# Making the low part of the MLP's downward weights with an accumulating DMA instead of VectorE

## The chip, the cores and the metric

One core of one Trainium2 chip runs the whole program. The metric is the time of one execution in microseconds, as the device measures it; several runs are made and the median is given. A profile of one further execution shows what each engine did and when.

## The reference

One inference step of a decoder trunk with two layers, for a prompt of 512 tokens and 8 samples of 4 new tokens each (544 token columns in all), model width 1024. Layer 0 mixes tokens by sparse attention, layer 1 by retention, and each layer ends in an MLP:

```python
def sqrelu_mlp(h, w1, w2):
    return jnp.square(jax.nn.relu(h @ w1)) @ w2
...
        yp = yp + sqrelu_mlp(rms_norm(yp, ln_mlp[i]), mlp_w_in[i], mlp_w_out[i])
        ys = ys + sqrelu_mlp(rms_norm(ys, ln_mlp[i]), mlp_w_in[i], mlp_w_out[i])
```

`mlp_w_in` is 1024 x 4096 and `mlp_w_out` is 4096 x 1024 for each layer, all in float32.

## The kernel before

All values are float32, while the matmuls read a rounded format, `fp32r`. To keep precision each operand is split in two: a high part, the value rounded to `fp32r`, and a low part, the value minus its high part. A product is then three matmuls: high by high, high by low, low by high. For weights these parts are called `wh` and `wl` (for the upward weights of the later chunks `sh` and `sl`), for activations `hs` or `xs`.

**The MLP.** The hidden width of 4096 is cut into 8 chunks of 512. For each chunk the upward product makes 512 hidden rows, which are squared, split and kept in `H[c]`; the downward product takes them back to 1024 rows and adds those to the residual `x` (L640). The upward product of chunk 0 uses plain blocks, that of the other chunks uses `fast_block`, which needs fewer products (its matmuls are at L554). The downward product of a chunk is `dense4`: two calls of `block`, 512 columns each, and each gives two units of 256 columns. So a chunk has four downward units, called here its **first to fourth quarter**. One quarter is 48 matmuls at L490: two tiles of 128 columns, for each four steps along the hidden rows, and in each step four matmuls on `wh` and then two on `wl`. The units of a chunk stand in this order: first half of the next chunk's upward product, quarters one and two, second half of the upward product, quarters three and four. After the last chunk's upward product only quarters are left.

**A quarter's weights.** One load of 1 MB (`raw`, L462, issued by SP) brings the weights of two quarters. `split_w` then takes a quarter's view of `raw`: ACT copies it into `wh` (L449), and VectorE subtracts `wh` from it into `wl` (L450). `wh` and `wl` have two buffers each (`bufs=2`). So the split of a quarter can start only when TensorE has finished the quarter two before it. `raw` has four buffers; one is free for the next load when the split of its second view is through.

**Who sets the order.** `run` hands out the split of a unit ahead of its matmuls, by a lead of about 9 us of estimated TensorE time, and a scheduler then puts each engine's instructions in one fixed order. Each engine runs its list in that order and waits on semaphores. TensorE too waits in order: where a `wl` is late, everything behind that matmul is late.

POOL has little to do in the MLP: at the end of a layer it adds up squares for the next norm (L396, L398).

Of the kernel before, what the change touches and what calls it, by code (L numbers as in the profile page):

```python
# [26 lines left out]
FT = mybir.dt.float32  # L27
# [3 lines left out]
AF = mybir.ActivationFunctionType  # L31
OP = mybir.AluOpType
# [111 lines left out]
def decoder_step(ctx, tc, x_prompt, x_sample, cache_k, cache_v, cache_kidx, state_ret, page_table,  # L144
# [5 lines left out]
    V, A, G, PE, SY = nc.vector, nc.scalar, nc.gpsimd, nc.tensor, nc.sync  # L150
# [9 lines left out]
    def ps_mm():  # L160
        return psum.tile([128, 2, 512], FT, name="mm", tag="mm")
# [7 lines left out]
    def raw_tile():  # L169
        return wp.tile([128, 2048], FT, name="raw", tag="raw", bufs=4)  # L170

    def open_main(st, name, early, hs=None):
        pool = st.enter_context(tc.tile_pool(name=name, bufs=1))
        PS.update(main=pool, early=early, hs=hs or (pool, "hs", 16))
        return pool
# [5 lines left out]
    def hs_tile(dt=FR):  # L181
        return row_tile("hs", dt)
# [14 lines left out]
    def halves(ps, rows=slice(0, 128)):  # L197
        return ps[rows, :, :HALF] if len(ps.shape) == 3 else two(ps[rows])

    def two(ap):  # L200
        return ap.rearrange("p (c n) -> p c n", c=2)
# [45 lines left out]
    def settle():  # L247
        while follow or held:
            release()
            more()  # L250
# [129 lines left out]
    def start_norm(columns=False, then=None):  # L380
        norm["pending"] = True
        follow.append(finish_norm(columns, then))
# [40 lines left out]
    def combine(i, gi):  # L423

        lo, hi = slice(0, HALF), slice(HALF, T)
        x0, x1 = hs_tile(FT), hs_tile(FT)
        for k, x in ((2 * i, x0), (2 * i + 1, x1)):
            A.activation(x, xT[k], AF.Identity, scale=gains[:, gi * 8 + k:gi * 8 + k + 1])
        n, t = hs_tile(FT), hs_tile(FT)
        V.tensor_tensor(t[:, lo], x1[:, hi], x0[:, hi], op=OP.subtract)  # L430
        V.tensor_tensor(n[:, lo], x0[:, lo], x0[:, hi], op=OP.subtract)
        yield 0.9
        V.scalar_tensor_tensor(n[:, hi], n[:, lo], -1.0, x1[:, hi], op0=OP.mult, op1=OP.subtract)
        V.scalar_tensor_tensor(t[:, hi], n[:, hi], -1.0, x1[:, lo], op0=OP.mult, op1=OP.subtract)
        yield 0.9
        for src, names in ((t, ("t3", "t4")), (n, ("n1", "n2"))):
            h, l = xs_tile(), xs_tile()
            split_into(h, l, src)
            XC[i].update({names[0]: (h[:, lo], l[:, lo]), names[1]: (h[:, hi], l[:, hi])})
            yield 0.8  # L440


    def split_w(view, eng):
        nk, cols = view.shape[1], view.shape[2]
        wh = wp.tile([128, 1024], FR, name="wh", tag="wh", bufs=2)
        wl = wp.tile([128, 1024], FR, name="wl", tag="wl", bufs=2)
        h = wh[:, :nk * cols].rearrange("p (k c) -> p k c", k=nk)
        l = wl[:, :nk * cols].rearrange("p (k c) -> p k c", k=nk)
        A.activation(h, view, AF.Copy)  # L449
        eng.tensor_tensor(l, view, h.bitcast(FT), op=OP.subtract)  # L450
        return h, l

    def block(src, k0, nk, c0, cols, xs, evac, m=128, eng=None):


        raw = {}

        def view():
            if "v" not in raw:
                t = raw_tile()  # L460
                raw["v"] = t[:, :nk * cols].rearrange("p (k c) -> p k c", k=nk)
                SY.dma_start(raw["v"], src[128 * k0:128 * (k0 + nk), c0:c0 + cols]  # L462
                             .rearrange("(k p) c -> p k c", p=128))
            return raw["v"]
        per = max(1, min(cols // m, 8 // nk))

        def unit(u):
            got = {}

            def split():  # L470
                got["w"] = split_w(view()[:, :, m * per * u:m * per * (u + 1)], eng or V)
                yield nk * per * m / 128 * 0.75

            def parts():
                xx = xs() if callable(xs) else xs
                for t in range(per):
                    yield from tile_of(got["w"], xx, t, m, evac, per * u + t)
            return dict(load=view, split=split, parts=parts, rest=lambda: [])
        return [unit(u) for u in range(cols // (m * per))]

    def tile_of(hl, xs, t, m, evac, i):

        ps = ps_mm()
        n = len(xs)
        for k in range(n):
            xh, xl = xs[k]
            for w, xx in ((hl[0], (xh, xl)), (hl[1], (xh,))):
                for x in xx:
                    for c in range(2):
                        PE.matmul(ps[:m, c, :HALF], w[:, k, m * t:m * (t + 1)],  # L490
                                  x[c] if isinstance(x, tuple) else x[:, HALF * c:HALF * (c + 1)],
                                  start=(k == 0 and w is hl[0] and x is xh),
                                  stop=(k == n - 1 and w is hl[1]))
            if k % 2:
                if k == n - 1:
                    if norm["pending"]:
                        z = PS["main"].tile([128, T], FT, name="early", tag=PS["early"][0], bufs=PS["early"][1])
                        A.activation(two(z), halves(ps), AF.Copy)
                        ps = z
                    held.append((evac, i, ps))  # L500
                    release()
                yield 1.5
# [127 lines left out]
    def dense8(src, c0, cols, evac, m=128, eng=None):  # L630
        return block(src, 0, 8, c0, cols, XS, evac, m, eng)

    def dense4(src, k0, xs, evac, eng=None):

        return block(src, k0, 4, 0, 512, xs, evac, eng=eng) + \
            block(src, k0, 4, 512, 512, xs, lambda m, ps: evac(m + 4, ps), eng=eng)

    def add_to_x(done=None):
        def evac(m, ps):
            V.tensor_tensor(two(xT[m]), halves(ps), two(xT[m]), op=OP.add)  # L640
            if done:
                return done(m)
        return evac

    def split_into(dst_h, dst_l, src):
        A.activation(dst_h, src, AF.Copy)  # L646
        V.tensor_tensor(dst_l, src, dst_h.bitcast(FT), op=OP.subtract)  # L647
# [4 lines left out]
    if True:  # L652
# [7 lines left out]
        for k in range(KT):  # L660
            ps = ps_mm()
            for b in range(4):
                src = xin[k // 2][b // 2][:, b % 2, 128 * (k % 2):128 * (k % 2 + 1)]
# [523 lines left out]
    def mlp(l, done):  # L1187
        with ExitStack() as st:
            mp = open_main(st, f"mlp{l}", ("r", 4), PS["hs"])
            start_norm()  # L1190
            H = {}

            def hidden(c, r):
                A.activation(r, r, AF.Square)  # L1194
                hh, hl = hs_tile(), hs_tile()
                split_into(hh, hl, r)
                H[c].append((hh, hl))

            def ev_first(i, ps):
                r = mp.tile([128, T], FT, name="r", tag="r", bufs=4)  # L1200
                V.scalar_tensor_tensor(two(r), halves(ps), 0.0, two(RB), op0=OP.max, op1=OP.mult)
                hidden(0, r)

            def up(c):
                H[c] = []

                def ev(i, r, ps):
                    if i == 0:
                        V.scalar_tensor_tensor(r[:, :HALF], r[:, :HALF], 0.0, RB[:, :HALF], op0=OP.max, op1=OP.mult)
                        V.scalar_tensor_tensor(r[:, HALF:], ps, 0.0, RB[:, HALF:], op0=OP.max, op1=OP.mult)  # L1210
                    else:
                        V.scalar_tensor_tensor(r, r, 0.0, RB, op0=OP.max, op1=OP.mult)
                    hidden(c, r)
                return fast_block(mlp_w_in[l], 512 * c, ev) + fast_block(mlp_w_in[l], 512 * c + 256, ev)

            n = DFF // 512
            H[0] = []
            units = block(mlp_w_in[l], 0, 8, 0, 256, XP, ev_first) + \
                block(mlp_w_in[l], 0, 8, 256, 256, XP, ev_first)
            gens = [combine(i, 2 + l) for i in range(KT // 2)]  # L1220
            side.append([gens, 1.0, 0.0])

            def combined():
                drain(gens)
                side.clear()
            for c in range(n):
                down = dense4(mlp_w_out[l], 4 * c, lambda c=c: H[c], add_to_x(done if c == n - 1 else None))
                nxt = up(c + 1) if c + 1 < n else []
                if c == 0:
                    nxt[0]["before"] = combined  # L1230
                units += nxt[:1] + down[:2] + nxt[1:] + down[2:]
            run(units)
            settle()
# [339 lines left out]
```

## Time and profile before

| what | value |
|---|---|
| median of 3 runs | 1600.4 us (1598.68 to 1602.14) |
| the profiled execution | 1602.17 us, its span 1600.4 us |
| TensorE busy | 1552.9 us, 97% of the span |
| VectorE busy | 1067.6 us, 67% |
| ACT busy | 611.7 us, 38% |
| POOL busy | 195.8 us, 12% |
| mean granted TensorE clock | 0.989 of full speed |
| moved by DMA | 172.53 MB, mean 108 GB/s |

The span runs from the first instruction to the last; the time of the execution has 1.8 us more around it. An engine's share is busy time alone: what an engine waits for, and who waits for it, stands in other views. The two MLPs take about 293 to 677 us and 1227 to 1594 us of the span, close to half of it.

### The profile page before, as it was taken

How to read it: one execution, taken by the hardware profiler on the slowest of the kernel's cores; microseconds unless marked ns; L12 is line 12 of the kernel's file. 1: busy time of each engine (PE TensorE's matmuls, PEld its weight loads, DVE VectorE, ACT ScalarE, POOL GpSimd, SP SyncE). 2: the span in 40 equal slices, each digit the busy share in tenths (PEclk: the TensorE clock that was granted, in tenths of full speed). 3: DMA queues.
4: the chain of work that ended last, by engine and by line, in shares of the span. 5: the costliest groups of instructions: out<-in, count | busy, mean ns of one | idle time of the engine just before them, and what ended most of it. 6: DMA issues, size and time to landing. Idle time of an engine off the chain costs nothing.

```text
span 1600.4 us, 27988 instructions
## 1 busy us (share of the span) xinstructions
PE 1552.9 (97%) x11578; PEld 1443.7 (90%) x11578; DVE 1067.6 (67%) x1946; ACT 611.7 (38%) x1030; POOL 195.8 (12%) x180
## 2 busy tenths in 40 slices
PE   7989899889999999999999999999998999999998
PEld 6789459889999999998898899899898999999998
DVE  5599774877777676656465565564668776777663
ACT  4323563454444344423132232132235544444332
POOL 3211320300000000312211121122112000000000
PEclk9899999999999999999999999999999999999999
DMA  6432243222332232223724522622632313332211
GB/s 174 150 99 85 74 162 106 73 74 92 106 99 85 81 106 97 76 89 112 237 67 144 195 77 99 228 89 80 237 93 80 106 54 106 106 106 80 80 54 57
DMA packets 135774, 172.53 MB, mean 108 GB/s; under 512 B 11660, under 2 KB 92630, under 8 KB 135646
## 3 DMA queue, kind: packets, MB, share of 16 engines
q1 hardware_dynamic: 135578, 170.72, 32.8%
q8 instruction: 91, 1.49, 0.4%
q14 instruction: 37, 0.30, 0.1%
q10 hardware_dynamic: 68, 0.02, 0.0%
HBM read 148.34 MB, written 25.01 MB: 108 GB/s over the span
## 4 chain that ended last, share of the span: by engine, by line
PE 89%; DVE 8%; ACT 2%; DMA 1%; issue 1%; ACTq 0%; DVEq 0%
PE mm L490 56%; PE mm L554 16%; PE pa L554 2%; PE pb L1456 2%; PE pa L1427 2%; PE pb L1482 1%; PE pa L1404 1%; PE pb L1437 1%; DVE wl L450 1%; PE pa L998 1%; PE pa L1025 1%; DMA raw<-in_mlp_w_in_dram 1%; PE mm L1096 1%; DVE sl L647 1%; DVE x L640 1%
## 5 line engine op out<-in xcount | busy, mean ns | idle before, releaser
L490 PE MATMUL mm<-xs,wh 128*128 128x272 f32 (+1 forms) x2784 | 501.9, 295 | 9.2 <-ACT r L1194 4.3
L490 PEld LDWEIGHTS mm<-xs,wh 128*128 128x128 f32 (+1 forms) x2784 | 410.1, 191 | 32.2 <-issue 16.9
L490 PE MATMUL mm<-hs,wh 128*128 128x272 f32 x2304 | 394.6, 290 | 8.1 <-DVE x L640 5.4
L490 PEld LDWEIGHTS mm<-hs,wh 128*128 128x128 f32 x2304 | 330.5, 189 | 10.9 <-DVE hs L647 3.4
L449 ACT ACTIVATE wh<-raw 128x1024 fp32r<-128x1024 f32 x159 | 167.9, 1057 | 397.2 <-PE mm L490 378.9
L490 PE MATMUL mm<-xs,wl 128*128 128x272 f32 (+1 forms) x1392 | 300.8, 293 | 0.6 <-DVE wl L450 0.6
L554 PE MATMUL mm<-xs,sh 128*128 128x272 f32 x1344 | 260.6, 289 | 3.3 <-DVE xs L647 0.8
L490 PE MATMUL mm<-hs,wl 128*128 128x272 f32 x1152 | 241.3, 289 | 0.0
L640 DVE TENSOR_TENSOR x<-mm,x 128x544 f32<-128x544 f32 x176 | 126.9, 723 | 156.7 <-PE mm L490 155.7
L490 PEld LDWEIGHTS mm<-xs,wl 128*128 128x128 f32 (+1 forms) x1392 | 223.5, 190 | 8.5 <-issue 5.6
L554 PEld LDWEIGHTS mm<-xs,sh 128*128 128x128 f32 x1344 | 210.5, 188 | 7.2 <-ACT r L570 4.3
L450 DVE TENSOR_TENSOR wl<-raw,wh 128x1024 fp32r<-128x1024 f32 x151 | 193.4, 1282 | 21.1 <-ACT wh L449 12.9
L554 PE MATMUL mm<-xs,sl 128*128 128x272 f32 x672 | 193.2, 287 | 0.0
L490 PEld LDWEIGHTS mm<-hs,wl 128*128 128x128 f32 x1152 | 182.3, 189 | 0.2
L554 PEld LDWEIGHTS mm<-xs,sl 128*128 128x128 f32 x672 | 126.5, 188 | 0.0
L646 ACT ACTIVATE sh<-ss 128x512 fp32r<-128x512 f32 x112 | 70.6, 630 | 136.8 <-PE mm L554 133.5
L647 DVE TENSOR_TENSOR sl<-ss,sh 128x512 fp32r<-128x512 f32 x112 | 77.9, 696 | 21.0 <-PE mm L554 21.0
L646 ACT ACTIVATE sh<-raw 128x512 fp32r<-128x512 f32 x84 | 53.0, 631 | 88.4 <-PE mm L554 69.0
L1439 DVE SCALAR_TENSOR_TENSOR raw<-raw,pb 128x512 f32<-128x512 f32 x64 | 43.4, 684 | 34.3 <-PE pb L1437 25.5
L647 DVE TENSOR_TENSOR sl<-raw,sh 128x512 fp32r<-128x512 f32 x84 | 58.6, 698 | 9.1 <-PE mm L554 9.1
L647 DVE TENSOR_TENSOR hs<-r,hs 128x544 fp32r<-128x544 f32 x64 | 46.1, 721 | 18.9 <-ACT hs L646 18.8
L396 POOL COPY acc<-sq 128x544 f32<-128x544 f32 x4 | 3.2, 800 | 434.4 <-ACT sq L394 434.4
(341 smaller groups left out, 1841.1 us busy)
## 6 DMA issues: line engine op xcount, KB each, us to landing
raw<-in_mlp_w_in_dram SPq DMA_DIRECT2D x32, 1024.0 KB
raw<-in_mlp_w_out_dram SPq DMA_DIRECT2D x32, 1024.0 KB
raw<-in_ret_w_in_dram SPq DMA_DIRECT2D x24, 1024.0 KB
raw<-in_state_ret_dram SPq DMA_DIRECT2D x32, 512.0 KB
out_dram<-raw SPq DMA_DIRECT2D x32, 512.0 KB
raw<-in_ret_w_out_dram SPq DMA_DIRECT2D x8, 1024.0 KB
raw<-in_att_w_in_dram SPq DMA_DIRECT2D x7, 1024.0 KB
raw<-in_cache_k_dram SPq DMA_DIRECT2D x32, 128.0 KB
```

Of the source, the lines that this page charges most:

```text
L449: A.activation(h, view, AF.Copy)
L450: eng.tensor_tensor(l, view, h.bitcast(FT), op=OP.subtract)
L490: PE.matmul(ps[:m, c, :HALF], w[:, k, m * t:m * (t + 1)], x[c] if isinstance(x, tuple) else x[:, HALF * c:HALF * (c + 1)], start=(k == 0 a ...
L554: PE.matmul(ps, a[:, i, :], b, start=(first and i == 0 and j == 0), stop=(i == 3 and j == 2), skip_group_check=True)
L640: V.tensor_tensor(two(xT[m]), halves(ps), two(xT[m]), op=OP.add)
L646: A.activation(dst_h, src, AF.Copy)
L647: V.tensor_tensor(dst_l, src, dst_h.bitcast(FT), op=OP.subtract)
L998: PE.matmul(ps[:, :W], qT[h][:, 128 * blk:128 * (blk + 1)], kT[h // 4][:, :W], start=True, stop=True)
L1025: PE.matmul(po[:, 128 * j:], vtok[:, j, 128 * (h // 4):128 * (h // 4 + 1)], PT[j], start=(j == 0), stop=(j == 3))
L1427: PE.matmul(po[32 * j:32 * (j + 1), :], qa[:, dt, bb, j, :], S0[j // 2][:, j % 2, dt, :], start=(bb == 0 and dt == 0), stop=False, skip_gr ...
L1439: V.scalar_tensor_tensor(sl, sl, gam4[h], pu, op0=OP.mult, op1=OP.add)
L1456: PE.matmul(ps[:, SP - WJ[j]:], v[:, j, 128 * e:128 * (e + 1)], a[:, AM[j]:AM[j] + WJ[j]], start=(j == 0 and v is vh and a is am[0]), stop ...
```

## The change

For the downward weights of both MLPs, and for nothing else, `wl` is made in another way. ACT writes `wh` as before, and then writes the view times -1, rounded to `fp32r`, into `wl`, which is `wh` negated. Then POOL issues a DMA that reads the quarter's weights from HBM a second time and adds them to what stands in `wl`. The subtraction on VectorE goes. There are 64 quarters (2 layers, 8 chunks, 4 quarters), so 64 VectorE instructions go, and 64 ACT instructions and 64 DMAs of 512 KB come. The plain load of `raw` by SP stays.

```diff
-    def split_w(view, eng):
+    def split_w(view, eng, again=None):
...
         A.activation(h, view, AF.Copy)
-        eng.tensor_tensor(l, view, h.bitcast(FT), op=OP.subtract)
+        if again is None:
+            eng.tensor_tensor(l, view, h.bitcast(FT), op=OP.subtract)
+        else:
+            A.activation(l, view, AF.Copy, scale=-1.0)
+            G.dma_start(l, again, accum_op=OP.add)
         return h, l
...
+        def here(lo, hi):
+            return src[128 * k0:128 * (k0 + nk), c0 + lo:c0 + hi].rearrange("(k p) c -> p k c", p=128)
...
             def split():
-                got["w"] = split_w(view()[:, :, m * per * u:m * per * (u + 1)], eng or V)
+                lo, hi = m * per * u, m * per * (u + 1)
+                got["w"] = split_w(view()[:, :, lo:hi], eng or V, here(lo, hi) if by_dma else None)
...
-                down = dense4(mlp_w_out[l], 4 * c, lambda c=c: H[c], add_to_x(done if c == n - 1 else None))
+                down = dense4(mlp_w_out[l], 4 * c, lambda c=c: H[c], add_to_x(done if c == n - 1 else None), by_dma=True)
```

The lines of the changed kernel are 1 to 8 higher than before: ACT's `wh` is L450 there, its negated copy L454, POOL's DMA L455.

ACT's list in a middle chunk, around the split of a fourth quarter (`hs<-r` splits hidden rows, `sh` is the upward weights' high part, `r<-mm` empties an upward product); before:

```order
L646 ACTIVATE hs<-r 128x544
L449 ACTIVATE wh<-raw 128x1024
L646 ACTIVATE sh<-raw 128x512
L564 ACTIVATE r<-mm 128x272
L646 ACTIVATE sh<-ss 128x512
L567 ACTIVATE r<-mm 128x272
L449 ACTIVATE wh<-raw 128x1024
```

and now:

```order
L654 ACTIVATE hs<-r 128x544
L450 ACTIVATE wh<-raw 128x1024
L454 ACTIVATE wl<-raw 128x1024
L654 ACTIVATE sh<-raw 128x512
L572 ACTIVATE r<-mm 128x272
L654 ACTIVATE sh<-ss 128x512
L575 ACTIVATE r<-mm 128x272
L450 ACTIVATE wh<-raw 128x1024
L454 ACTIVATE wl<-raw 128x1024
```

The negated copy stands right behind `wh`, here and in 60 of the 64 quarters; the rest of ACT's list is as it was.

POOL's list from layer 0's MLP to the start of layer 1 (`acc` are the sums of squares, `qarr` and `atsr` belong to the retention); before:

```order
L396 COPY acc<-sq 128x544
L398 TENSOR_TENSOR acc<-sq,acc 128x544 x6
L1259 MEMSET qarr_7772 128x512
L1262 MEMSET atsr_7774 32x128
L1259 MEMSET qarr_7776 128x512
L1262 MEMSET atsr_7778 32x128
L398 TENSOR_TENSOR acc<-sq,acc 128x544
```

and now:

```order
L455 DMA wl<-in_mlp_w_out_dram 128x4x256 x31
L396 COPY acc<-sq 128x544
L398 TENSOR_TENSOR acc<-sq,acc 128x544 x2
L455 DMA wl<-in_mlp_w_out_dram 128x4x256
L398 TENSOR_TENSOR acc<-sq,acc 128x544 x4
L1267 MEMSET qarr_7804 128x512
L1270 MEMSET atsr_7806 32x128
```

All 32 DMAs of layer 0 are new on POOL; the last one stands between the sums of squares. In layer 1 the 32 stand alone. TensorE's list is almost the same: every quarter's first `wl` matmuls keep their place, but for layer 0's last chunk, where 12 upward matmuls come ahead of the first quarter's, and in the fourth quarter eight `wh` matmuls instead of four come ahead of the first `wl`.

## Rows read from the trace of the kernel before

**Rows 1.** Page, part 1: engine, busy us and share, instructions.
```profile
PE 1552.9 (97%) x11578; PEld 1443.7 (90%) x11578; DVE 1067.6 (67%) x1946; ACT 611.7 (38%) x1030; POOL 195.8 (12%) x180
```

**Rows 2.** Windows: start:end, length, busy us of each engine (instructions), granted clock, DMA.
```profile
280.00:330.00 50.00, 43.52 (x324) 42.59 (x323) 42.45 (x65) 27.49 (x46) 12.54 (x7) 0.93 0.20 64
...
380.00:430.00 50.00, 49.87 (x399) 49.65 (x398) 36.49 (x57) 21.97 (x37) 0.00 (x0) 1.00 0.33 106
```

**Rows 3.** Timeline of ACT and VectorE, third and fourth quarter's split: start, us, [idle before].
```profile
439.24 1.06 ACT L449 ACTIVATE wh<-raw 128x1024 fp32r<-128x1024 f32 x1 [2.25 <-PE mm L490]
...
449.76 1.06 ACT L449 ACTIVATE wh<-raw 128x1024 fp32r<-128x1024 f32 x1 [0.94 <-PE mm L490]
...
450.86 1.23 DVE L450 TENSOR_TENSOR wl<-raw,wh 128x1024 fp32r<-128x1024 f32 x1
```

**Rows 4.** Timeline of TensorE: second quarter's end, third's first `wl`, fourth's.
```profile
449.57 0.41 PE L490 MATMUL mm<-hs,wl 128*128 128x272 f32 x2
...
451.82 0.42 PE L490 MATMUL mm<-hs,wl 128*128 128x272 f32 x2
...
460.34 0.66 PE L490 MATMUL mm<-hs,wh 128*128 128x272 f32 x4
460.83 0.41 PE L490 MATMUL mm<-hs,wl 128*128 128x272 f32 x2
```

**Rows 5.** Groups by line: busy us, mean ns; and POOL's eight `wl`, ns min/median/max.
```profile
L449 ACT ACTIVATE wh<-raw 128x1024 fp32r<-128x1024 f32 x159 | 167.9, 1057 | 397.2 <-PE mm L490 378.9 <-issue 16.7 <-ACT sq L1473 0.9
L450 POOL TENSOR_TENSOR wl<-raw,wh x8: 2341/2385/2426, 38.6 to 119.8; 128x1024 fp32r<-128x1024 f32 x8
```

**Rows 6.** Timeline of SP: issues of one lone load, and of two together.
```profile
430.87 0.37 SPq L462 DMA_DIRECT2D raw<-in_mlp_w_out_dram  x1
452.11 0.37 SPq L516 DMA_DIRECT2D raw<-in_mlp_w_in_dram  x1
452.71 0.39 SPq L462 DMA_DIRECT2D raw<-in_mlp_w_out_dram  x1
```

**Rows 7.** Windows over those loads; the last two numbers are DMA share and GB/s.
```profile
435.00:436.00 1.00, 1.00 (x10) 1.00 (x9) 0.89 (x2) 0.00 (x0) 0.00 (x0) 1.00 0.28 105
...
453.00:460.00 7.00, 7.00 (x58) 7.00 (x58) 2.73 (x6) 1.98 (x3) 0.00 (x0) 1.00 0.91 299
```

**Rows 8.** Timeline, end of layer 0: last two quarters' `wh`, first `wl` matmuls.
```profile
658.70 1.06 ACT L449 ACTIVATE wh<-raw 128x1024 fp32r<-128x1024 f32 x1 [1.86 <-PE mm L490]
...
665.28 1.06 ACT L449 ACTIVATE wh<-raw 128x1024 fp32r<-128x1024 f32 x1 [0.35 <-PE mm L490]
...
665.83 0.41 PE L490 MATMUL mm<-hs,wl 128*128 128x272 f32 x2
...
671.83 0.41 PE L490 MATMUL mm<-hs,wl 128*128 128x272 f32 x2
```

**Rows 9.** Window at the end of layer 0, columns as in rows 7.
```profile
671.00:672.00 1.00, 1.00 (x10) 1.00 (x10) 0.47 (x1) 0.73 (x1) 1.00 (x1) 1.00 0.94 320
```

**Rows 10.** Timeline, end of layer 1: last quarter's `wh`, first `wl` matmul.
```profile
1579.47 1.06 ACT L449 ACTIVATE wh<-raw 128x1024 fp32r<-128x1024 f32 x1 [2.90 <-PE mm L490]
...
1587.69 0.41 PE L490 MATMUL mm<-hs,wl 128*128 128x272 f32 x2
```

**Rows 11.** Timeline of VectorE, first chunk of layer 0.
```profile
320.87 1.22 DVE L450 TENSOR_TENSOR wl<-raw,wh 128x1024 fp32r<-128x1024 f32 x1 [3.32 <-ACT wh L449]
322.01 0.43 DVE L344 COPY RB<-pb 128x272 f32<-128x272 f32 x1
...
323.05 0.72 DVE L1201 SCALAR_TENSOR_TENSOR r<-early,RB 128x544 f32<-128x544 f32 x1
```

**Rows 12.** Timeline of TensorE, first chunk of layer 0, and window behind its first wait.
```profile
324.55 0.56 PE L490 MATMUL mm<-xs,wh 128*128 128x272 f32 x1 [2.15 <-ACT r L1194]
...
338.44 0.52 PE L490 MATMUL mm<-hs,wh 128*128 128x272 f32 x2 [1.79 <-DVE hs L647]
...
324.50:327.50 3.00, 2.95 (x13) 2.98 (x14) 1.86 (x3) 3.00 (x6) 0.00 (x0) 0.50 0.00 0
```

More of the change, by code (lines that the diff above doesn't have):

```diff
@@ L449, in split_w, with block @@
         A.activation(h, view, AF.Copy)
-        eng.tensor_tensor(l, view, h.bitcast(FT), op=OP.subtract)
+        if again is None:
[3 more added lines that the diff above has]
+            G.dma_start(l, again, accum_op=OP.add)
         return h, l
-    def block(src, k0, nk, c0, cols, xs, evac, m=128, eng=None):
+    def block(src, k0, nk, c0, cols, xs, evac, m=128, eng=None, by_dma=False):
         raw = {}
@@ L461, in view @@
                 raw["v"] = t[:, :nk * cols].rearrange("p (k c) -> p k c", k=nk)
-                SY.dma_start(raw["v"], src[128 * k0:128 * (k0 + nk), c0:c0 + cols]
-                             .rearrange("(k p) c -> p k c", p=128))
+                SY.dma_start(raw["v"], here(0, cols))
             return raw["v"]
+        def here(lo, hi):
+            return src[128 * k0:128 * (k0 + nk), c0 + lo:c0 + hi].rearrange("(k p) c -> p k c", p=128)
         per = max(1, min(cols // m, 8 // nk))
@@ L631, in dense8, with dense4 @@
         return block(src, 0, 8, c0, cols, XS, evac, m, eng)
-    def dense4(src, k0, xs, evac, eng=None):
-        return block(src, k0, 4, 0, 512, xs, evac, eng=eng) + \
-            block(src, k0, 4, 512, 512, xs, lambda m, ps: evac(m + 4, ps), eng=eng)
+    def dense4(src, k0, xs, evac, eng=None, by_dma=False):
+        return block(src, k0, 4, 0, 512, xs, evac, eng=eng, by_dma=by_dma) + \
+            block(src, k0, 4, 512, 512, xs, lambda m, ps: evac(m + 4, ps), eng=eng, by_dma=by_dma)
     def add_to_x(done=None):
```

## The prediction

> **What bounds the kernel now.** I read the page's busy shares first. TensorE works 1552.9 of 1600.4 us, VectorE 1067.6, ACT 611.7, POOL 195.8 [rows 1]. TensorE is the bound, so an edit pays only where TensorE stands still. That is why the windows come next: in the middle of an MLP TensorE is busy 49.87 us of 50 while VectorE has 36.49, and only in a layer's first chunk does it lose time, 6.5 us of 50, with VectorE at 42.45 [rows 2]. In the middle, then, taking 1.2 us off VectorE per quarter pays nothing. What can change there is a wait: a `wl` that comes too late for TensorE.
>
> So the quantity to read is the margin of each quarter. It runs from the moment its split may start (TensorE has left the buffer) to its first `wl` matmul. Take a middle chunk. The second quarter's last matmuls start at 449.57; the fourth quarter's split waits for them, and ACT begins at 449.76 [rows 3, 4]. VectorE follows at 450.86 with 1.23 us [rows 3], so `wl` is ready at 452.1. TensorE wants it at 460.83 [rows 4]. VectorE's way is early by 8.7 us, and nobody waits for it.
>
> **The change, part by part.**
>
> *ACT.* 64 negated copies of the same form as `wh`, 1.06 us each by the group's mean of 1057 ns [rows 5]: 68 us on an engine that has 28 us free in each 50 [rows 2]. They stand directly behind `wh`. Behind them on ACT wait the next split of upward weights and the emptying of an upward product. Those are done ahead of need in the middle chunks, where ACT itself mostly waits for TensorE. I take 0, with 0 to 5 us as bounds: were that cover gone, each could cost its 1.06 us.
>
> *VectorE.* 64 subtractions go, 1.22 us each. Hidden in the middle; in the first chunk of a layer two of the four stand in the stretch that TensorE waits for. One of them, at 320.87, holds up the copy of `RB` at 322.01 and with it the hidden rows at 323.05 [rows 11], for which TensorE (through ACT) waits until 324.55 [rows 12]. But ACT's own half of that copy now stands behind a negated copy, so I count 1 us per layer instead of 2.4: a gain of 2, bounds 0 to 4.9 (four times 1.22).
>
> *The margin with the DMA.* Now ACT takes two steps, and what is left of the margin, from the end of the negated copy to the first `wl` matmul, must hold POOL's issue, the transfer and its landing. Call the length of these three L. For the fourth quarter: 449.76 + 1.06 + 1.06 = 451.88, to 460.83: **8.9 us** [rows 3, 4]. For the third: 439.24 + 2.12 = 441.36, to 451.82: 10.5 us [rows 3, 4]. First and second quarters have more than 14. The pattern of the fourth quarter stands in 11 of 16 chunks; the first one or two of each layer have 11 us or more there, and the last chunks are different.
>
> *The last chunk.* No upward product stands between its quarters, so the split of one has only one other quarter to hide behind. Layer 0: third quarter 658.70 + 2.12 = 660.82, to 665.83, 5.0 us; fourth 665.28 + 2.12 = 667.40, to 671.83, plus 0.5 for the four more `wh` matmuls that now come first: 4.9 us [rows 8]. In layer 1 transposes of the output stand between: 1579.47 + 2.12 = 1581.59, to 1587.69, 6.1 us for the fourth quarter [rows 10]. POOL's list is no hindrance: in front of the one DMA that stands among the sums of squares are sums of earlier tiles.
>
> *L itself.* No POOL-issued DMA of weights and no adding DMA is in this trace, so L is bounded by the nearest rows. A lone load of 1 MB is issued at 430.87 [rows 6] and its last quarter-window of traffic ends at about 435.3 (105 GB/s in the window 435 to 436, a quarter of full rate) [rows 7]: 4.4 us, of which some 3.1 are data. The adding DMA moves half as many bytes, but must read the weights and the old `wl` both, so I take the same 3.1 us of data; below that stands 1.6 us, half. The Trainium skill says the same of an adding transfer ("Collectives: The Full Stack", section "The bandwidth ceiling"): it needs two source reads, and the reads set its rate. No run here shows it. For the issue, SP's rows have 0.37 us [rows 6], the floor; the nearest row on POOL itself is its own `wl` of the same tile, 2.39 us [rows 5]. Building the list for 512 rows in software is closer to the second: I take 2.4, so 2.0 more than SP. **L alone: 4.4 + 2.0 = 6.4 us**, bounds 2.8 to 10.
>
> *L beside loads.* The split that frees a `raw` buffer also lets SP's next load go. Two loads of 1 MB are issued at 452.11 and 452.71 [rows 6], just when the fourth quarter's DMA would be, and they keep the DMA engines at 0.91 for 7 us, 453 to 460 [rows 7]. Nine of the 11 fourth quarters have two loads beside them. If the two queues take turns, the 3.1 us of data last 6.2: **L = 6.4 + 3.1 = 9.5 us**, plus 0.4 as the loads start first: 9.9. If the loads go first altogether and POOL takes twice 2.4, it is 16; without sharing, 6.4.
>
> *The sum.* Middle: 9.9 - 8.9 = 1.0 us late, nine times: 9. End of layer 0: a load beside it too (0.94 of the DMA engines busy in 671 to 672) [rows 9]: 9.9 - 4.9 = 5.0; the third quarter's 6.4 - 5.0 = 1.4 is within that, since the fourth's need moves with it. End of layer 1, alone: 6.4 - 6.1 = 0.3. Thirds: 10.5 holds 6.4. First chunks: -2. Together 9 + 5 + 0.3 - 2 = **+12 us**. On the profiled execution's 1602.2 (span 1600.4 and 1.8 around it) that is 1614; on the median, 1600.4, **1613 us**.
>
> **The rivals.**
>
> *A, hidden.* If POOL issues in 1.4 us or less, or the turn-taking costs the small transfer less than its own length again, L beside loads is under 8.9 and the middle is clean. What is left is 0 to 3 us at the end of layer 0, and -2: 1598 to 1602, no measurable change. For it: 8.9 is large beside the 4.4 us of a whole 1 MB load. Against it: the nine coincidences with loads. By the skill's page "DMA: Bandwidth & Descriptors" ("Anatomy of one DMA - SWDGE (gpsimd) path") a POOL-issued DMA takes 2.0 us and its bytes at 436 GB/s, an estimate of 3.2 us here; by that alone this rival holds and the time is 1598. The same page ("Issuing engines are not separate DMA queues") says that transfers from all issuers interleave on the same 16 engines, which speaks for turns, and so against the change. No run here shows either for POOL.
>
> *B, long.* Generating or adding is slow: L of 14 beside loads and 11 to 12 alone, from twice POOL's 2.4 and data at half the rate that I take. Then each of 11 fourth quarters waits 2 to 5 us, and the clock joins in: after a wait of 2.15 us at 324.55 TensorE's granted clock is 0.50 of full speed, its lower level of 1.2 GHz, for 3 us, with 13 matmuls in place of 24, 1.4 us lost; after a wait of 1.79 us at 338.44 the next matmuls run at full pace [rows 12]. Nine times (5.1 + 1.4) and twice (2.6 + 1.4) is 66, the two ends 9 + 6, less 2: 1680. It sets in where L passes 11. For it: POOL does its list in software, and no row bounds that from above.
>
> *C, faster.* The other side: L is hidden as in A, and VectorE's relief is worth all of its four subtractions in the first chunks: up to -4.9, 1595.5 to 1597. For it, VectorE's 42.45 of 50 us there [rows 2]. Against it: half of the chain in that stretch runs over ACT, which gets longer. It decides only if every margin holds.
>
> That the change does not do what it says is no rival: the order shows the 64 subtractions gone.
>
> **How the numbers follow.** A change of 0.2%, 3.2 us, is about what a measurement of this kernel can tell from none. Forecast (middle waits of 0.2 to 2.1 us, +4 to +30): 0.42, its own range 1604 to 1630. A, within 3.2 us: 0.20. C, faster by more: 0.12. B: 0.26. So faster 0.12, same 0.20, slower 0.68. The range must leave out no more than 0.2: from 1597, which leaves out about half of C (0.06), to 1675, which leaves out half of B (0.13).
>
> **What would show it.** Right: rows of TensorE that wait for the DMA into `wl` about 1 us in front of fourth quarters, with two loads beside, none in front of first and second ones, and 3 to 6 us at the end of layer 0; POOL's issue near 2.4 us; VectorE's busy time down by 78 us, ACT's up by 68. Wrong: no waits for `wl` at all (A, C), or waits above 2 us with clock windows at 0.50 behind them, in third quarters too (B); an ACT row that TensorE waits for in each chunk would upset the zero for ACT.

## The result, and the profile after

The changed kernel takes **1643.44 us** (median of 4 runs, 1640.69 to 1645.71), the kernel before beside it 1599.54 us: the ratio is **1.0275**, 95% interval 1.0255 to 1.0296. So 44 us were lost where 12 were forecast. The profiled execution took 1645.60 us, its span is 1643.7.

Page, part 1 of the changed kernel, and three groups of its part 5 (columns as in [rows 1] and [rows 5]; the last part of a group is the engine's idle time in front of it and what ended most of that):

```profile
PE 1567.2 (95%) x11578; PEld 1452.8 (88%) x11578; DVE 991.4 (60%) x1882; ACT 664.0 (40%) x1094; POOL 276.9 (17%) x244
...
L498 PE MATMUL mm<-hs,wl 128*128 128x272 f32 x1152 | 247.8, 295 | 32.2 <-DMA wl<-in_mlp_w_out_dram 32.1
...
L455 POOL DMA_DIRECT2D wl<-in_mlp_w_out_dram x64 | 82.3, 1285 | 675.5 <-ACT wl L454 599.9
...
L454 ACT ACTIVATE wl<-raw 128x1024 fp32r<-128x1024 f32 x64 | 66.7, 1042 | 0.0
```

The work moved as the diff says: VectorE's busy time falls by 76 us, ACT gains 67 us in copies (52 in busy time), POOL gains 81. TensorE now waits 32.1 us for the new DMA, at the `wl` matmuls. Its own busy time rose too, by 14.3 us, with the same 11578 matmuls: some of them ran slower.

The waits of TensorE (total us, times, longest), and the line of POOL's DMA (duration ns min/median/max; at the end, the time from issue to landing):

```profile
PE mm L498 <- DMA wl<-in_mlp_w_out_dram: 32.1, 13, 3.2
PE mm L498 <- DVE x L648: 8.1, 11, 2.1
...
L455 POOL DMA_DIRECT2D wl<-in_mlp_w_out_dram x64: 1273/1282/1441, 321.0 to 1624.7; - x64
...
DMA to landing us min/median/max: 5.6/6.0/12.1
```

The first row of waits did not exist before. POOL needs 1.28 us to issue one DMA, and it always does; the time to landing runs from 5.6 to 12.1 us. What makes the difference is to be seen in one middle chunk. The timeline of its fourth quarter, the one whose margin [rows 3, 4] give:

```profile
446.78 1.04 ACT L454 ACTIVATE wl<-raw 128x1024 fp32r<-128x1024 f32 x1
447.85 0.37 SPq L524 DMA_DIRECT2D raw<-in_mlp_w_in_dram  x1
448.12 1.28 POOL L455 DMA_DIRECT2D wl<-in_mlp_w_out_dram  x1 [9.26 <-ACT wl L454]
448.31 0.53 SPq L467 DMA_DIRECT2D raw<-in_mlp_w_out_dram  x1
...
456.39 0.66 PE L498 MATMUL mm<-hs,wh 128*128 128x272 f32 x4
...
459.80 0.82 PE L498 MATMUL mm<-hs,wl 128*128 128x272 f32 x2 [2.75 <-DMA wl<-in_mlp_w_out_dram]
```

ACT ends the negated copy at 447.82. That copy is the last reader of `raw`, so it releases POOL's DMA and SP's next load in the same instant, and a second load was waiting in SP's list behind the first. All three are issued within half a microsecond. TensorE could have gone on at 457.05; it goes on at 459.80.

The traffic of the two queues in single microseconds of this stretch, 450 to 451, 452 to 453, 453 to 454, 455 to 456 and 458 to 459 (q1 carries SP's loads, q0 POOL's DMA; packets, MB, share of the 16 engines):

```profile
q1 hardware_dynamic: 268, 0.27, 91.2%
...
q1 hardware_dynamic: 338, 0.37, 107.9%
...
q1 hardware_dynamic: 162, 0.28, 84.1%
q0 software_dynamic: 39, 0.04, 24.6%
...
q1 hardware_dynamic: 95, 0.19, 57.8%
q0 software_dynamic: 89, 0.09, 56.2%
...
q0 software_dynamic: 96, 0.09, 54.8%
q1 hardware_dynamic: 13, 0.02, 7.0%
```

Up to 453 only loads move. POOL's packets begin 5 us after the issue, then alternate with the second load's, one to one, and are alone only when both loads are through. A quarter without loads beside it reads otherwise. The third quarter of this chunk is issued at 437.58, and its traffic begins in the window 439 to 440 and is over by 443:

```profile
437.58 1.28 POOL L455 DMA_DIRECT2D wl<-in_mlp_w_out_dram  x1 [15.61 <-ACT wl L454]
...
439.00:440.00 1.00, 1.00 (x11) 1.00 (x10) 0.73 (x1) 0.04 (x1) 0.00 (x0) 1.00 0.44 34
440.00:441.00 1.00, 1.00 (x11) 1.00 (x10) 0.00 (x0) 0.00 (x0) 0.00 (x0) 1.00 1.08 156
...
443.00:444.00 1.00, 1.00 (x11) 1.00 (x10) 1.00 (x3) 0.67 (x2) 0.00 (x0) 1.00 0.00 0
```

Landing comes 5.8 us after issue. Read over all 64 DMAs, the time to landing goes in steps: 5.6 to 6.3 us with no load beside, 8.0 to 9.9 with one, 10.8 to 12.1 in the fourth quarters with two (in the first two chunks of a layer, where the loads stand otherwise, up to 11.9). A load's own data are worth about 3 us here: q1 takes 32.4% of 1643.7 us for 170.72 MB, 3.3 us for 1 MB. So each load beside it delays the DMA by about 3 us, its own length.

**Behind the waits.** Windows of 2 to 3 us directly behind three such waits (columns as in [rows 2]; the third number from the end is the granted clock):

```profile
459.80:462.00 2.20, 2.20 (x9) 2.20 (x10) 0.00 (x0) 0.00 (x0) 0.00 (x0) 0.50 1.19 186
560.20:563.20 3.00, 2.96 (x23) 2.97 (x24) 0.16 (x1) 0.00 (x0) 0.00 (x0) 1.00 0.83 131
657.60:660.60 3.00, 3.00 (x13) 3.00 (x14) 0.00 (x0) 0.00 (x0) 0.00 (x0) 0.51 1.09 162
```

After waits of 2.75 and 1.94 us the clock granted is 0.50 of full speed, the lower level of 1.2 GHz; after one of 3.12 us it is 1.00. Of the twelve waits for the DMA that last 1.9 us or more, eight were followed by such a spell.

**Where the 43 us of span are.** The starts of one matmul in both kernels, the first on `wl` of the quarter named, from the timelines of TensorE:

| place | before | after | difference |
|---|---|---|---|
| last product with `wl` ahead of layer 0's MLP | 301.78 | 300.51 | -1.27 |
| end of layer 0's first chunk (its fourth quarter) | 371.48 | 367.43 | -4.05 |
| third chunk, third quarter | 451.82 | 447.87 | -3.95 |
| seventh chunk, fourth quarter | 642.52 | 657.60 | +15.08 |
| layer 0's last quarter | 671.83 | 695.79 | +23.97 |
| last such product ahead of layer 1's MLP | 1214.05 | 1238.90 | +24.85 |
| layer 1's first quarter | 1247.24 | 1269.58 | +22.35 |
| layer 1, second chunk, third quarter | 1319.28 | 1342.34 | +23.06 |
| layer 1's last chunk, first quarter | 1564.64 | 1607.40 | +42.76 |
| end of the span | 1600.40 | 1643.74 | +43.34 |

Within the MLPs only the first chunks gained; both middles lost about 19 us, the end of layer 0 about 9, the end of layer 1 nothing.

### The profile page after: what moved, and what is told of

Same layout as the page of the kernel before. It is cut to its first block, busy times and chain, and to the rows that moved or that the text cites. A ratio compares the mean times of both kernels' runs of the same rounds, so it can differ in the third digit from the quotient of the medians.

```text
span 1643.7 us, 28180 instructions
## 1 busy us (share of the span) xinstructions
PE 1567.2 (95%) x11578; PEld 1452.8 (88%) x11578; DVE 991.4 (60%) x1882; ACT 664.0 (40%) x1094; POOL 276.9 (17%) x244
## 3 DMA queue, kind: packets, MB, share of 16 engines
q1 hardware_dynamic: 135578, 170.72, 32.4%
q0 software_dynamic: 33792, 33.56, 13.3%
## 4 chain that ended last, share of the span: by engine, by line
PE 50%; issue 30%; DMA 9%; DVE 8%; POOL 2%; ACT 1%; POOLq 0%; ACTq 0%; DVEq 0%
PE mm L498 34%; DMA wl<-in_mlp_w_out_dram 8%; POOL wl L455 2%; PE pb L1464 2%; PE pa L1435 2%; PE mm L562 1%; PE pb L1490 1%; PE pa L1412 1%; PE pb L1445 1%; PE pa L1006 1%; PE pa L1033 1%; DVE sc L773 1%; DVE xs L410 1%; PE mm L1104 1%; DVE wl L452 1%
## 5 line engine op out<-in xcount | busy, mean ns | idle before, releaser
L498 PE MATMUL mm<-hs,wh 128*128 128x272 f32 x2304 | 400.9, 294 | 5.4 <-DVE x L648 4.1
L498 PEld LDWEIGHTS mm<-hs,wh 128*128 128x128 f32 x2304 | 336.6, 193 | 8.3 <-DVE x L648 2.4
L450 ACT ACTIVATE wh<-raw 128x1024 fp32r<-128x1024 f32 x159 | 167.9, 1057 | 395.0 <-PE mm L498 376.8
L498 PE MATMUL mm<-hs,wl 128*128 128x272 f32 x1152 | 247.8, 295 | 32.2 <-DMA wl<-in_mlp_w_out_dram 32.1
L498 PEld LDWEIGHTS mm<-hs,wl 128*128 128x128 f32 x1152 | 187.1, 194 | 35.4 <-DMA wl<-in_mlp_w_out_dram 35.2
L455 POOL DMA_DIRECT2D wl<-in_mlp_w_out_dram x64 | 82.3, 1285 | 675.5 <-ACT wl L454 599.9
L452 DVE TENSOR_TENSOR wl<-raw,wh 128x1024 fp32r<-128x1024 f32 (+1 forms) x87 | 115.2, 1326 | 9.5 <-ACT wh L450 7.8
L454 ACT ACTIVATE wl<-raw 128x1024 fp32r<-128x1024 f32 x64 | 66.7, 1042 | 0.0
```

Of the source, the lines that this page charges most:

```text
L454: A.activation(l, view, AF.Copy, scale=-1.0)
L455: G.dma_start(l, again, accum_op=OP.add)
L498: PE.matmul(ps[:m, c, :HALF], w[:, k, m * t:m * (t + 1)], x[c] if isinstance(x, tuple) else x[:, HALF * c:HALF * (c + 1)], start=(k == 0 a ...
```

## The experiments

The **theory** after this reading: the loads that the same split sets free go ahead of the adding DMA, L grows to 12 in fourth quarters, and the clock adds to it. The **rivals**: the fourth quarter is late by its place or because adding is slow; the loss is spread over all quarters (more HBM traffic, ACT's longer list); three transfers at once share whoever comes first. The first line number of each diff is left out; all diffs are against the changed kernel unless said otherwise.

| run | us, median | before beside it | ratio | 95% interval |
|---|---|---|---|---|
| e1_hold | 1603.11 | 1599.10 | 1.0026 | 1.0010 to 1.0042 |
| e2_sbuf | 1604.46 | 1599.10 | 1.0028 | 1.0012 to 1.0044 |
| e3_noadd | 1611.28 | 1599.10 | 1.0084 | 1.0062 to 1.0107 |
| e4_q123 | 1604.76 | 1599.10 | 1.0037 | 1.0021 to 1.0053 |
| e5_nodma | 1594.77 | 1598.92 | 0.9971 | 0.9956 to 0.9985 |
| e6_chunk0 | 1594.09 | 1598.92 | 0.9969 | 0.9956 to 0.9982 |
| e7_act_step | 1613.62 | 1598.92 | 1.0090 | 1.0067 to 1.0113 |
| e8_loads_behind | 1604.04 | 1598.92 | 1.0030 | 1.0015 to 1.0044 |
| e9_pool_chunk0 | 1607.30 | 1599.64 | 1.0044 | 1.0028 to 1.0060 |
| e10_q4_only | 1638.49 | 1599.64 | 1.0235 | 1.0213 to 1.0257 |
| e11_loads_behind_2 | 1590.32 | 1599.64 | 0.9938 | 0.9923 to 0.9952 |
| e12_loads_pool_only | 1596.94 | 1600.56 | 0.9982 | 0.9967 to 0.9997 |

**Loads issued only after the DMA has landed (`e1_hold`).**

```diff
             G.dma_start(l, again, accum_op=OP.add)
+            d = tmp.tile([128, 1], FT, name="hold", bufs=1)
+            G.tensor_tensor(d, view[:, 0, :1], l.bitcast(FT)[:, 0, :1], op=OP.subtract)
```

> The change, with one small POOL instruction more per quarter that reads raw and the landed wl (a subtraction of one column into a tile that nobody reads), so that the raw buffer comes free, and SP's next load is issued, only after the adding DMA has landed. Theory 1 (the loads that the same split sets free go ahead of the adding DMA): every L is 5.6 to 6.3 us as in the lone quarters, the middle margins of 9.2 us hold, no wait for the DMA is left but up to 0.7 us at the end of layer 0, no clock loss, and what stays is the first chunks' gain: 1596 to 1601 us. Theory 2 (the fourth quarter is late by its place, or the adding DMA is slow by itself there): the waits of 2 to 3 us in fourth quarters stay, 1635 to 1645 us. Theory 3 (the loads are now late in their turn): waits for raw, 1605 us or more.

It gave 1603.11 us: some 40 of the 44 us are back. The waits for the DMA fall from 32.1 us in 13 to 3.4 in 6. They are not quite gone, since one load stays beside some fourth quarters: the next upward one, whose buffer another split had freed; three of the six, 2.2 us, stand at the end of layer 0. It goes out 0.07 us behind POOL, and L is then 8.5 to 9.3 us, the length with one load:

```profile
496.70 1.32 POOL L455 DMA_DIRECT2D wl<-in_mlp_w_out_dram  x1 [4.33 <-ACT wl L454]
496.77 0.37 SPq L526 DMA_DIRECT2D raw<-in_mlp_w_in_dram  x1
...
506.00 0.52 PE L500 MATMUL mm<-hs,wl 128*128 128x272 f32 x2 [0.52 <-DMA wl<-in_mlp_w_out_dram]
```

The place is the same, one load is gone, and the wait is 0.5 in place of 2.8. That is against the rival of the place. The time is above the 1596 to 1601 that I expected; of the profiled execution's excess, 2.3 us stand ahead of layer 0's MLP (the last product with `wl` there starts at 304.09, not 301.78), where no weights are made by DMA.

The run also shows that the order of issue alone does not decide. The packets of the trace say when data begin to move: a load of SP's moves its first packet 1.0 us after its issue where nothing is in front of it, POOL's adding DMA 2.0 us after. So a load that SP issues half a microsecond behind the DMA still goes first, as in layer 0's first chunk:

```profile
334.84 1.31 POOL L455 DMA_DIRECT2D wl<-in_mlp_w_out_dram  x1 [4.13 <-ACT wl L454]
335.33 0.37 SPq L526 DMA_DIRECT2D raw<-in_mlp_w_in_dram  x1
```

The DMA's first packet comes 5.5 us after its issue there, and L is 10.1. Loads issued 2.2 to 2.4 us behind it, in the second chunks, cost it nothing: L is 5.5 to 5.8.

**The DMA reads `raw` in SBUF, not HBM (`e2_sbuf`).**

```diff
-            G.dma_start(l, again, accum_op=OP.add)
+            G.dma_start(l, view, accum_op=OP.add)
```

> The adding DMA reads the weights from raw in SBUF, not again from HBM. It reads raw, so raw comes free, and SP's next load is issued, only when it has landed; HBM traffic falls by 33 MB. Theory 1 (collision with the loads): L 5.6 to 6.3 everywhere, 1596 to 1601 us, as with the held buffer. If reading from SBUF is slower than from HBM, L passes 9 and the waits come back: above 1620 us. Theory 2 (place or adding): 1635 to 1645 us.

1604.46 us, the same as with the held buffer, and L is 5.4 to 10.6 with a median of 5.7 (6.0 in the changed kernel). `raw` is held here by the DMA itself. Twelve waits of at most 1.7 us remain, 9.2 us together, again above the expected range. The time to landing without a load is mostly 5.4 to 5.9 us where it was 5.6 to 6.3, so reading the weights from HBM costs the DMA about 0.3 us.

**The same DMA without adding (`e3_noadd`).** It overwrites the negated copy, so the subtraction is left out.

```diff
-            G.dma_start(l, again, accum_op=OP.add)
+            G.dma_start(l, again)
```

> The same DMA without the addition (it overwrites the negated copy, so the subtraction is left out and the low part is the whole weight). Theory 1: the lone L falls by what the second read costs, from 5.7 to 4.0 us if two reads set the data time (3.4 us of 16 engines each), and beside two loads it still lands behind them, about 10 us after issue: waits of about 1 us in ten fourth quarters, little or no clock loss, 1603 to 1612 us. If generating the descriptors sets L, it stays at 5.7 alone and 11.6 beside loads, 1640 us. If adding itself is what is slow beside loads, L is under 7 there and no wait is left: 1596 to 1600 us.

1611.28 us. The line of the DMA in this kernel:

```profile
L455 POOL DMA_DIRECT2D wl<-in_mlp_w_out_dram x64: 740/740/962, 319.5 to 1587.2; - x64
...
DMA to landing us min/median/max: 3.7/5.0/10.6
```

Without adding the issue is 0.74 us in place of 1.28, and the time to landing without a load about 3.9 in place of 5.8. The data take 2.2 us of all 16 engines (q0 has 8.7% of 1606.1 us, over 64) in place of 3.4 (13.3% of 1643.7). So adding costs 1.9 us per quarter. But beside two loads the plain DMA still lands 8.0 to 10.6 us after issue: the loads cost it 4 to 7 us, much as they cost the adding one 5 to 6. Nine waits of at most 1.7 us are left, and no spell of lower clock follows the longest two.

**First three quarters only (`e4_q123`).** VectorE's subtraction stays in fourth quarters and in the last chunk.

```diff
-... by_dma=True)
+... by_dma=c < n - 1 and (0, 1, 2))
```

> The DMA makes wl in the first three quarters of each chunk but the last; VectorE's subtraction stays in fourth quarters and in the last chunk of each layer. The loads collide with second quarters (8.5 to 10 us of L against 17 of margin) and no longer with a late one. Theory 1: no wait for the DMA is left; the first chunks' gain of 3 to 4 us stays in part: 1596 to 1600 us. Rival (the loss is the added HBM traffic or ACT's longer list in all quarters, not the late fourth quarter): three quarters of the loss stays, 1625 to 1635 us.

1604.76 us. The rival of a spread loss is out: 38 of 44 us are gone with 42 of 64 quarters still on the DMA. But my range is missed as well, by 5 us. The wait for the DMA is down to one of 0.3 us in a first chunk; what stands in its place is a wait for ACT:

```profile
PE mm L562 <- ACT r L578: 4.5, 12, 0.4
```

That wait is the emptying of an upward product behind ACT's longer list, 0.4 us in each of twelve chunks. The scheduler also put TensorE's matmuls in another order here (the first `wl` matmul of fourth quarters stands 12 matmuls further back), so the two are not separated.

**Fourth quarters only (`e10_q4_only`).** Chunks two to seven; everything else as before the change.

```diff
-... by_dma=True)
+... by_dma=0 < c < n - 1 and (3,))
```

> The complement: the DMA makes wl only in the fourth quarters of chunks two to seven (12 of 64 quarters), everything else as before. Theory 1 (the loss sits in these quarters: ten or eleven waits of 2 to 3 us, and about 1.6 us of lower clock behind some seven of them; no gain in the first chunks): 1630 to 1642 us. Rival (the loss is spread over all quarters with the DMA): 1600 to 1612 us.

1638.49 us, inside the range: 12 of 64 quarters bring 39 of the 44 us. One row of the waits says why:

```profile
PE mm L498 <- DMA wl<-in_mlp_w_out_dram: 24.2, 10, 3.0
```

Ten waits, 24.2 us, and behind eight of them a spell of lower clock, four of these twice as long as in the changed kernel (6.9 us in place of 3.4). So 24 us of waits cost 44 us in the two middles, where 27 cost 39 there.

**The loads issued by POOL, behind the DMA in its list (`e8_loads_behind`).** Same traffic, same place, the same split that frees the buffer. What differs is that the loads come behind the DMA, and that they go through POOL's queue instead of SP's (q0 carries 96.48 MB here, 33.56 in the changed kernel).

```diff
-                SY.dma_start(raw["v"], here(0, cols))
+                (G if by_dma else SY).dma_start(raw["v"], here(0, cols))
...
-                SY.dma_start(got["v"], src[:, c0:c0 + 256]...
+                (G if src.shape[1] == DFF else SY).dma_start(got["v"], src[:, c0:c0 + 256]...
```

> The change, with the MLP's 1 MB loads (upward and downward weights) issued by POOL, so that in its list they stand behind the adding DMA of the fourth quarter instead of on SP beside it. HBM traffic and its place in the chunk are the same. Theory 1 (what delays the DMA is that the loads' data go ahead of it): in fourth quarters L falls from 11 to 12 us to under 8, no wait over 1 us is left there, 1598 to 1606 us. Rival (the three transfers share the engines whoever is first, so that all end together): L stays at 9 to 12 us and the time above 1620 us.

1604.04 us. The rival of sharing expected L of 9 to 12 us here:

```profile
449.25 1.29 POOL L455 DMA_DIRECT2D wl<-in_mlp_w_out_dram  x1 [8.98 <-ACT wl L454]
450.02 1.44 POOL L524 DMA_DIRECT2D raw<-in_mlp_w_in_dram  x1
450.93 1.31 POOL L467 DMA_DIRECT2D raw<-in_mlp_w_out_dram  x1
...
458.00 0.41 PE L498 MATMUL mm<-hs,wl 128*128 128x272 f32 x2
```

Both loads follow within 1.7 us, yet L is 5.9 us and TensorE does not wait. Loads behind the DMA in its own queue do not delay it. A load behind it in SP's queue is another case: one issued 0.19 us behind shared the engines with it in the changed kernel, one issued 2.2 us behind cost it nothing with the held buffer. Middle fourth quarters land in 5.6 to 6.0 us, the seventh chunk's of layer 0 apart. Layer 1 has no wait over 0.1 us. All that is left, 7.2 us in three waits, is the end of layer 0, where the next stage's loads still come from SP.

**The same, with VectorE's subtraction in the last two chunks of each layer (`e11_loads_behind_2`).**

```diff
-... by_dma=True)
+... by_dma=c < n - 2)
```

> As with the loads issued by POOL, but VectorE's subtraction in the last two chunks of each layer, where the next stage's loads come from SP and two of the last quarters have only 8.9 us. Theory 1 (what was left of the loss, some 10 us, is the end of layer 0, beside SP's loads): no wait for the DMA is left, 1592 to 1597 us. Rival (loads issued by POOL cost something elsewhere): 1600 us or more.

1590.32 us, 0.62% faster than before, and better than the range. Not all of that is shown to come of the change: in the profiled execution, 12.0 us shorter in span than the one before, the first chunks hold 7.6 us, and 4.5 stand ahead of layer 0's MLP, where the clock was at its lower level for 10 us in place of 24. The DMA is gone from the waits, which now begin like this:

```profile
PE mm L498 <- DVE x L648: 6.8, 10, 1.5
```

**The loads on POOL without the change (`e12_loads_pool_only`).** VectorE subtracts everywhere, no negated copy, no adding DMA.

```diff
-                got["w"] = split_w(view()[:, :, lo:hi], eng or V, here(lo, hi) if by_dma else None)
+                got["w"] = split_w(view()[:, :, lo:hi], eng or V, None)
```

(against the version with the loads behind)

> The kernel before in its arithmetic (VectorE's subtraction everywhere, no adding DMA, no negated copy), with only the MLP's 1 MB loads issued by POOL in place of SP. It prices that part of the version with the loads behind. Theory (that part is worth nothing by itself, and the version's gain is VectorE's relief in first chunks): 1597 to 1601 us. Rival (the loads on POOL are themselves worth some us): 1592 to 1596 us.

1596.94 us, just under the lower edge of my range, ratio 0.9982, interval 0.9967 to 0.9997: a gain of 0.5 to 5 us. The profiled execution, the fastest of twelve, does not find it in the MLPs: of the 8.1 us by which its span is shorter, 6.8 stand ahead of layer 0's MLP, where the clock was at its lower level for 7 us in place of 24. Whether the loads on POOL have to do with that stays open.

**No DMA at all (`e5_nodma`).** The addition is left out; ACT's copies and VectorE's relief stay.

```diff
-            G.dma_start(l, again, accum_op=OP.add)
```

> The adding DMA left out altogether: wl is only the negated copy, so the addition of the weights is left out and the low part is wrong in value; ACT's 64 copies are added and VectorE's 64 subtractions gone as in the change. What is left is the relief of VectorE in first chunks against ACT's longer list. Theory 1 (ACT's copies cost nothing in the middle): the first chunks' gain alone, 1594.5 to 1597 us. Rival (ACT's copies hold up the emptying of upward products, as twelve waits of 0.4 us did where the DMA was kept out of fourth quarters): 1598 to 1603 us.

1594.77 us. VectorE's relief, less what ACT's copies cost, is worth 4 us. In the middle chunks the copies cost nothing measurable in this order of instructions: TensorE does not wait there for ACT.

**ACT's step alone, VectorE adding in place of the DMA (`e7_act_step`).**

```diff
-            G.dma_start(l, again, accum_op=OP.add)
+            eng.tensor_tensor(l, view, l.bitcast(FT), op=OP.add)
```

> ACT's negated copy as in the change, but VectorE adds the weights to it in place of the DMA: VectorE keeps 64 operations of the same length, ACT has its 64 more, and no DMA is added. This prices ACT's second step alone. Theory 1 (free in the middle chunks, 1 us at most in each first chunk): 1599 to 1603 us. Rival (ACT's list is a cost of its own in every chunk): 1604 to 1612 us, with TensorE waiting for ACT in middle chunks.

1613.62 us, a miss: 11 us above the theory's range and just above the rival's. The rival's sign is there too, TensorE waiting for ACT in middle chunks, as with the first three quarters only:

```profile
PE mm L562 <- ACT r L578: 5.1, 13, 0.5
```

By the matmuls of the table above, the first chunks lose 1.2 and 0.7 us against before, and what follows them 5.3 us in layer 0 and 5.0 in layer 1, about twice these waits. The run without the DMA has the same copies and no such wait. But the scheduler gave TensorE another order here, so whether the loss is that order's or comes of VectorE waiting for ACT's second step is not shown.

**First chunks only (`e6_chunk0`).**

```diff
-... by_dma=True)
+... by_dma=c == 0)
```

> The DMA only in the first chunk of each layer (8 of 64 quarters), VectorE's subtraction elsewhere. In the changed kernel's trace the first chunks gained about 2.8 and 2.5 us and no quarter there waited for the DMA by more than 0.3 us. Theory 1: that gain stays, 1594.5 to 1597 us. Rival (the gain is given back, because TensorE's order shifts or the second chunk starts with less done ahead): 1598 to 1602 us.

1594.09 us, 0.31% faster than before. The wait of 2.15 us at 324.55 in [rows 12] is 1.20 here:

```profile
322.61 0.36 PE L498 MATMUL mm<-xs,wh 128*128 128x272 f32 x1 [1.20 <-ACT r L1202]
```

and the spell of lower clock behind it is gone. Eight of the 64 quarters hold all of the relief that the run without the DMA showed.

**First chunks on POOL, no DMA (`e9_pool_chunk0`).** Against the kernel before:

```diff
-... add_to_x(done if c == n - 1 else None))
+... add_to_x(done if c == n - 1 else None), eng=G if c == 0 else None)
```

> The kernel before, with POOL's subtraction in place of VectorE's in the first chunk of each layer (8 quarters); no negated copy and no added DMA. POOL's subtraction of this tile takes 2.39 us where VectorE's takes 1.23, so wl is ready 1.2 us later, against margins of 8 us and more. Theory (the gain of the first chunks is VectorE's relief): 1592 to 1596 us, as with the DMA in first chunks. Rival (the gain needs the DMA or the other order of instructions): 1598 to 1602 us.

1607.30 us, slower by 0.44%: a miss for the theory as written, and a lesson of its own. VectorE is relieved of the subtraction and gets slower:

```profile
323.38 2.37 POOL L450 TENSOR_TENSOR wl<-raw,wh 128x1024 fp32r<-128x1024 f32 x1 [14.19 <-ACT wh L449]
...
323.97 2.37 DVE L1201 SCALAR_TENSOR_TENSOR r<-early,RB 128x544 f32<-128x544 f32 x1
```

The operation of VectorE beside POOL's takes 2.37 us; it took 0.72 in [rows 11]. The Trainium skill has this ("SBUF — State Buffer", section "Who interferes with whom"): an operation of VectorE with two inputs in SBUF contends with one of POOL that reads SBUF. The row agrees. Beside the DMA's issue on POOL nothing of the kind shows: in the changed kernel VectorE's operations of this form take 0.71 to 0.72 us there as elsewhere. So this run does not test whether relief alone brings the gain; the run without the DMA does.

## Why the prediction was right or wrong, point by point

**The way it goes, and the place.** Right: slower, by waits for the DMA into `wl`, in middle fourth quarters with two loads beside, and at the end of layer 0, none at the end of layer 1. Fourth quarters alone bring 39 of the 44 us, and moving the loads behind the DMA removes the middle's loss. So the mechanism is shown; the size was off by more than three times.

**The margin.** Forecast 8.9 us in a middle fourth quarter; measured 9.2, from the copy's end at 447.82 to 457.05, where TensorE stood ready.

**L alone.** Forecast 6.4 us from the copy's end; measured about 0.3 to POOL's start and 5.6 to 6.3 from there. The parts were off against each other: 1.28 us on POOL where I took 2.4, and 3.4 us of data where I took 3.1. The page of the Trainium skill that I weighed gives an estimate of 3.2 us for such a transfer ("DMA: Bandwidth & Descriptors", section "Anatomy of one DMA — SWDGE (gpsimd) path"), and neither kind measured here agrees: 3.9 us plain, 5.8 adding.

**L beside loads: the step that failed.** "If the two queues take turns, the 3.1 us of data last 6.2: L = 6.4 + 3.1 = 9.5 us, plus 0.4 as the loads start first: 9.9." Measured: 0.3 to POOL's start and 10.8 to 12.1 from there. The queues do take turns, packet by packet, but only with the second load. The first had gone through when the DMA's first packet moved, 5.2 us after issue instead of the 2.0 of a lone quarter; SP's load was quicker to its first packet, and why the DMA took turns with the second load and not with the first, no run shows. So the two loads cost the DMA 5 to 6 us, not 3.5. The sentence of the Trainium skill on interleaving ("DMA: Bandwidth & Descriptors", section "Issuing engines are not separate DMA queues") holds for the second load (89 packets to 95 in one microsecond), not for the first. The delay of 1.9 us on 9.9 is small, but what counts is L less the margin: 2.7 us in place of 1.0.

**The clock.** A second term was missing from the likeliest sum. I took waits of 1.0 us to leave the clock alone, as the one of 1.79 us in [rows 12] did, so I had its loss only in the rival of the long DMA. Waits of 1.9 to 3.2 us brought eight spells at the lower level. From the fourth quarter's first `wl` matmul to the next quarter's, TensorE lost another 1.6 us behind a wait with a spell (475.85 - 460.83 before, 476.38 - 459.80 after: 1.56) and 0.1 behind one without. Seven such at about 1.6 and 0.9 at the end of layer 0 are 12 us.

**The sum, with what was measured.** Middle waits: ten where I had nine, 27 us where I had 9. (Nine was a miscount: in the trace of before, ten of the 11 fourth quarters with this margin have two loads beside them, all but layer 1's seventh chunk.) End of layer 0: 2.0 in the second quarter and 3.1 in the fourth, 5.1 where I had 5.0, though I had put it into the fourth alone. End of layer 1: 0.03 where I had 0.3. Clock: 12 where I had 0. First chunks: about -2.8 and -1.8 where I had -2 together. In the span that is 32.1 (all waits for the DMA) + 12 - 4.6 = 39.5 us. Each wait also costs TensorE 0.17 us more than its length, since matmuls that follow at once overlap (2.92 us lost at 459.80 for a wait of 2.75): 13 times, 2.2. Some 2 us more stand at the end of layer 0, where TensorE's order changed a little, and 1.3 were gained ahead of the first MLP, which the change does not touch: 42.4 of 43.3.

**ACT at nothing.** Right for the middle of the changed kernel, shown without the DMA. In two other orders, TensorE waited 0.4 us in some twelve chunks for the emptying that I had named as the cover's weak point, and lost more than these waits; the zero holds for one order of instructions only.

**The rivals.** Hidden (A) is what remains where no load stands ahead. Faster (C) was right in its mechanism: first chunks alone gain 4.8 us. Long (B), priced at 66 us in the middle chunks from late landings and the clock, was the rival that came nearest in how the time is lost; its cause, a slow list on POOL, is refuted by the 1.28 us.

## What to carry to other kernels

A buffer that comes free can release a prefetch and a transfer that somebody needs in the same instant. Here the prefetch was quicker to its first packet (1.0 us against 2.0), even when issued a little later, and the needed transfer took its own time and about that of each load beside it: so put the prefetch behind it in the same queue, or hold the buffer. Price such a wait as the difference of two large times, and add the clock's part: here 1.6 us stood behind eight of twelve waits of 1.9 to 3.2 us. And take work off an engine only in the stages where another waits for it: here 8 of 64 quarters.

## What the runs showed of the hardware that was not expected

- Issued between SP's two loads, 0.27 us behind the first, POOL's DMA moved no packet for 5 us while that load was in flight; with no load beside it the first packets come 2.0 us after the issue. Loads of SP's move their first packet after 1.0 us.
- Adding costs a DMA of 512 KB 1.9 us: 0.54 on POOL (1.28 against 0.74) and 1.2 in the data (3.4 against 2.2).
- The length of a wait alone does not tell whether the clock falls behind it: 1.94 us did it, 3.12 us did not, in the same kernel.
- VectorE's operation of 0.72 us took 2.37 beside a subtraction on POOL.
